# Attention on one core: a rounded one-pass product for the row maxima, exact scores by keys, and the maxima brought in by small transfers

## The chip, the cores and the metric

The kernel runs on one core of a Trainium2 chip. A core has TensorE (PE, the matrix engine, with its weight loads PEld), VectorE (DVE), ScalarE (ACT), GpSimd (POOL) and SyncE (SP, which here only issues transfers), and 16 DMA engines. The metric is device time in microseconds of one execution, the median of several runs. The profiles are one execution each.

## The reference, cut to what matters

Two layers of a streaming encoder over 512 tokens of width 1024. Each layer is a half-weighted SwiGLU block, a mixing stage, a second SwiGLU block and a norm. The change is in the mixing stage, in the attention:

```
q = rms_norm(c_q) @ w_uq            # 8 heads of 64 + 32 (rotary)
kv = rms_norm(c_kv) @ w_ukv         # 8 heads of 64 (keys) + 64 (values)
q, k = rope(rms_norm(q)), rope(rms_norm(concat(k_nope, k_pe)))
for i in range(4):                  # blocks of 128 queries, keys up to the block's end
    scores = (q_i @ k.T) * 96 ** -0.5
    scores = where(chunk(key) <= chunk(query), scores, -1e30)   # chunks of 64 tokens
    out_i = softmax(scores) @ v
x = x + concat(attention, conv) @ w_out
```

Beside the attention runs a conv module: a gated product of 512 channels, a causal depthwise convolution of 31 taps, a layer norm over the channels and a swish. Its output is the other half of the input of `w_out`.

## The kernel before

Activations lie features by tokens: 128 partitions of features, 512 tokens along the free dimension. Most products are split: each float32 operand is cast to a rounded form (`FR`, the "hi") and the rest (the "lo"), and `mm3` (lines 151 to 154) sums hi x hi, hi x lo and lo x hi in PSUM. The mixing stage (`mix_body`, from line 609) works in this order in the code: two conv input groups, latents of queries and keys, `queries` and `keys` (which leave q and kn as tokens x heads x 100 numbers, 96 features and 4 marks for the mask), then the attention, then the conv taps, the layer norm and the output projection.

Attention goes head by head through five stages with a lag each, from `ORDER = "t0s1p3v4o5"` (lines 58 and 874): in step n come `turn(n)`, `scores(n-1)`, `turn_p(n-3)`, `values(n-4)` and `turn_out(n-5)`.

- `turn` transposes q and kn of a head on PE (lines 804, 809), and ScalarE and VectorE scale them out of PSUM as plain float32 (lines 806, 811).
- `scores` multiplies them in float32 with queries as rows: four blocks of 128 queries by 128, 256, 384 and 512 keys (line 824). VectorE takes each row's negated maximum (line 825), ScalarE the exponential with that maximum as bias (line 829). The marks add -1e30 where a query may not see a key.
- `turn_p` transposes the ten 128x128 blocks of the probabilities on PE (line 843); VectorE copies two of the three results out, ScalarE one (line 846, `EVP = "DAD"`).
- `values` multiplies by the values and a column of ones in float32 (line 854), VectorE divides (lines 860, 861).
- `turn_out` turns two heads at a time back and splits them into hi and lo (lines 871, 872, 158, 159).

The convolution has four channel groups (`CONV = "DAAD"`): two are 30 multiply-adds each on VectorE (line 894), two are 30 products on ScalarE (line 898) that POOL adds (line 902). Most of POOL's adds are queued behind the last step of `keys`. POOL then sums the four groups (lines 916 to 918); a product with `onesm` on PE (line 920) gives the mean, and the layer norm follows (lines 924 to 939: VectorE subtracts and adds squares, PE sums at line 190, POOL takes a power at line 170, PE spreads the result at line 208, VectorE and ScalarE finish, and the result is split). The output projection takes eight output groups; the attention half of the first three (`WOG`) is done in `early_groups` (lines 908 to 912), with weights of the first four loaded ahead (`WOP`).

The code fixes what is computed on which engine. The order in which each engine meets its instructions is made by the tile framework's scheduler: it takes ready instructions by their place in the code, with its own estimate of times and with the buffers that are free (seven PSUM banks, 40 slots of the ring that holds q, k and probabilities). `tc.issue_after(ins)` holds instructions of a block behind `ins` where both are on the same engine; `early_groups` is held behind `heads[H - 1]["s"]`, the last score matmul.

Of the kernel before, what the change touches and what calls it, by code (L numbers as in the profile page):

```python
# [7 lines left out]
FP = mybir.dt.float32  # L8
FR = mybir.dt.float32r
BF = mybir.dt.bfloat16  # L10
I32 = mybir.dt.int32
AF = mybir.ActivationFunctionType
ALU = mybir.AluOpType
AX = mybir.AxisListType

P = 128
D = 1024
S = 512
L = 2
KD = D // P  # L20
NT = S // P
H = 8
DN = 64
DR = 32
DQ = DN + DR
DM = DQ + 4
DV = 64
QL = 384
KVL = 256
# [14 lines left out]
LATE = ((), (), (), (0, 1, 2, 3), (4, 5, 6, 7))  # L44
SEQ = "q0 R c1 q1 q2 qo k kt tt uq uk c2"
POOLW = "wo"
QFOLD = 0
EARLY = "s"
PRELOAD = 1
WARM = 8  # L50
# [3 lines left out]
E3 = 3  # L54
WOG = 3
WOP = 4
EVP = "DAD"
ORDER = "t0s1p3v4o5"

VECS = [("g1", 8), ("gm", 8), ("g2", 8), ("gp", 8), ("gql", 3), ("gkl", 2),  # L60
        ("cw", 4 * CK), ("cb", 4), ("lg", 4), ("lb", 4), ("gq", 1), ("gk", 1)]
# [11 lines left out]
def encoder_kernel(ctx: ExitStack, tc: tile.TileContext, xT, consts, vecs, rgain, wgu1, wd1,  # L73
                   wcv, wql, wkl, wuq, wkv, wout, wgu2, wd2, wend, gend, out):
    nc = tc.nc
    PSUM = bass.MemoryType.PSUM
    cpool = ctx.enter_context(tc.tile_pool(name="const", bufs=1))
# [4 lines left out]
    small = ctx.enter_context(tc.tile_pool(name="small", bufs=2))  # L82
# [4 lines left out]
    def nm(s):  # L87
        uid[0] += 1
        return f"{s}{uid[0]}"

    def slot(dt=FP, w=S):
        return ring.tile([P, w], dt, tag="r", name=nm("r"))

    def tmp(w=S, dt=FP):
        return tmps.tile([P, w], dt, tag="t", name=nm("t"))

    def bank():
        return psum.tile([P, S], FP, tag="ps", name=nm("ps"))

    def tiny(tag, w, dt=FP):  # L100
        return small.tile([P, w], dt, tag=tag, name=nm(tag))

    V, A, G, T = nc.vector, nc.scalar, nc.gpsimd, nc.tensor
# [7 lines left out]
    ident = cst[:, CID:CID + P]  # L111
# [11 lines left out]
    V.memset(minus_half, -0.5)  # L123
    onesm = cpool.tile([P, P], FP, name="onesm")
    V.memset(onesm, 1.0 / CW)
    marks = cpool.tile([P, 2, NT, NT], FP, name="marks")
    G.memset(marks, 0.0)
    for t in range(NT):
        G.memset(marks[0:64, 0, t, t:t + 1], 1.0)
        G.memset(marks[64:P, 1, t, t:t + 1], -1e30)  # L130

    def vv(l, name):
        o, w = VOFF[name]
        return vec[:, l, o:o + w]
# [16 lines left out]
    def mm3(o, lh, ll, rh, rl, first, last, free=False):  # L151
        T.matmul(o, lh, rh, start=first, stop=False, skip_group_check=free)  # L152
        T.matmul(o, lh, rl, start=False, stop=False, skip_group_check=free)  # L153
        T.matmul(o, ll, rh, start=False, stop=last, skip_group_check=free)  # L154
# [7 lines left out]
    def split_scaled(src, scale, w=S, p=P):  # L162
        hi, lo = slot(FR, w), slot(FR, w)
        A.activation(hi[:p], src, AF.Copy, scale=scale)
        V.scalar_tensor_tensor(lo[:p], src, scale, hi[:p].bitcast(FP), ALU.mult, ALU.subtract)
        return hi, lo

    def rsqrt(y, ve):

        return G.tensor_tensor(y, ve, minus_half[:, 0:y.shape[1]], ALU.pow).ins  # L170
# [434 lines left out]
    def mix(l, gx, norm, done):  # L605
        with tc.tile_pool(name="k", bufs=4) as kpool:
            mix_body(kpool, l, gx, norm, done)

    def mix_body(kpool, l, gx, norm, done):
# [24 lines left out]
        cqT, ckT, pq, scqs = [], [], [], []  # L634
# [4 lines left out]
        ck = kpool.tile([P, NT, KW], FP, tag="ck", name=nm("ck"), bufs=1)  # L639
        q = kpool.tile([P, NT, H, DM], FP, tag="q", name=nm("q"), bufs=1)  # L640
        kn = kpool.tile([P, NT, H, DM], FP, tag="kn", name=nm("kn"), bufs=1)
        for side, v in enumerate((q, kn)):
            G.tensor_copy(v[:, :, :, DQ:DM], marks[:, side, :, None, :].to_broadcast([P, NT, H, NT]))
        cq, wkl_, sk, ckc, ratio = (tiny(n, NT) for n in ("cq", "wkl", "sk", "ckc", "ratio"))
        ssh = small.tile([P, NT, H], FP, tag="ssh", name=nm("ssh"))
        ssk = small.tile([P, NT, H], FP, tag="ssk", name=nm("ssk"))
# [78 lines left out]
        def queries():  # L725
            wq = [load_w(wuq[l, :, k * 768:(k + 1) * 768], 768, "uq") for k in range(3)]
            for t in range(NT):
                for hf in range(2):
                    hs = slice(hf * 4, hf * 4 + 4)
                    ps = bank()  # L730
                    for k in range(3):
                        ts_ = slice(t * P, (t + 1) * P)
                        cs = slice(hf * 384, (hf + 1) * 384)
                        mm3(ps[:, :384], cqT[k][0][:, ts_], cqT[k][1][:, ts_],
                            wq[k][0][:, cs], wq[k][1][:, cs], k == 0, k == 2)
                    A.copy(q[:, t, hs, 0:DQ], ps[:, :384].rearrange("p (h d) -> p h d", h=4))
                    j = tmp()
                    A.activation(j[:, :384], ps[:, :384], AF.Square)
                    V.tensor_reduce(ssh[:, t, hs], j[:, :384].rearrange("p (h d) -> p h d", h=4),
                                    axis=AX.X, op=ALU.add)  # L740
                V.tensor_scalar(ssh[:, t], ssh[:, t], cq[:, t:t + 1], None, ALU.add)
                scq = small.tile([P, H], FP, tag="scq", name=nm("scq"), bufs=5)
                rsqrt(scq, ssh[:, t])
                scqs.append(scq)
                if t % 2:
                    rope(q[:, t - 1:t + 1, :, DN:DQ], tabs[0][:, :, t - 1:t + 1], H)
                    if not QFOLD:
                        for i in (t - 1, t):
                            V.tensor_tensor(q[:, i, :, 0:DQ], q[:, i, :, 0:DQ], scqs[i][:, :, None].to_broadcast([P, H, DQ]),
                                            ALU.mult)  # L750

        def keys():
            wk = [load_w(wkv[l, :, k * WC:(k + 1) * WC], WC, "uk") for k in range(2)]
# [41 lines left out]
        at = []  # L795
        gq, gk = vv(l, "gq")[0:DM], vv(l, "gk")[0:DM]
        gqs = tiny("gqs", 1)
        V.tensor_scalar(gqs[0:DM], gq, DQ ** 0.5, None, ALU.mult)
        heads = [{} for _ in range(H)]

        def turn(h):
            ps = bank()
            for t in range(NT):
                T.transpose(ps[0:DM, t * P:(t + 1) * P], q[:, t, h], ident)
            qT = slot()
            A.activation(qT[0:DM], ps[0:DM], AF.Copy, scale=gqs[0:DM])
            ps = bank()
            for t in range(NT):
                T.transpose(ps[0:DM, t * P:(t + 1) * P], kn[:, t, h], ident)
            kT = slot()  # L810
            V.tensor_scalar(kT[0:DM], ps[0:DM], gk, None, ALU.mult)
            heads[h]["qk"] = qT, kT

        def scores(h):
            qT, kT = heads[h]["qk"]
            b01, b2, b3 = bank(), bank(), bank()
            mx = small.tile([P, NT], FP, tag="mx", name=nm("mx"), bufs=3)
            pi = []
            ps = [slot() for _ in range(3)]
            ps = [ps[0][:, 0:128], ps[0][:, 128:384], ps[1][:, 0:384], ps[2]]  # L820
            for i in range(NT):
                n = (i + 1) * P
                o = (b01[:, 0:128], b01[:, 128:384], b2[:, 0:384], b3)[i]
                heads[h]["s"] = T.matmul(o, qT[0:DM, i * P:(i + 1) * P], kT[0:DM, 0:n], start=True, stop=True).ins  # L824
                V.tensor_reduce(mx[:, i:i + 1], o, axis=AX.X, op=ALU.max, negate=True)
                p = ps[i]
                if QFOLD:
                    V.tensor_tensor(mx[:, i:i + 1], mx[:, i:i + 1], scqs[i][:, h:h + 1], ALU.mult)
                A.activation(p, o, AF.Exp, bias=mx[:, i:i + 1], scale=scqs[i][:, h:h + 1] if QFOLD else 1.0)  # L829
                pi.append(p)  # L830
            heads[h]["p"] = pi

        def turn_p(h):

            pi = heads[h]["p"]
            pt = []
            for js, eng in (((0,), EVP[0]), ((1, 3), EVP[1]), ((2,), EVP[2])):
                ps = bank()
                sb = slot()
                o = 0  # L840
                for j in js:
                    for i in range(j, NT):
                        heads[h]["t"] = T.transpose(ps[:, o:o + P], pi[i][:, j * P:(j + 1) * P], ident).ins  # L843
                        o += P
                    pt.append((j, sb[:, o - (NT - j) * P:o]))
                (A.copy if eng == "A" else V.tensor_copy)(sb[:, 0:o], ps[:, 0:o])
            heads[h]["pt"] = [p for _, p in sorted(pt, key=lambda e: e[0])]

        def values(h):

# [13 lines left out]
        def turn_out(h):  # L864
# [6 lines left out]
                T.transpose(ps[:, t * P:(t + 1) * P], o[:, t * P:(t + 1) * P], ident)  # L871
            at.append(split(ps))

        STAGES = [({"t": turn, "s": scores, "p": turn_p, "v": values, "o": turn_out}[c], int(d)) for c, d in zip(ORDER[::2], ORDER[1::2])]
        for step in range(H + 6):
            for stage, lag in STAGES:
                if 0 <= step - lag < H:
# [8 lines left out]
        for c in range(4):  # L886
# [4 lines left out]
            for k in range(CK - 2, -1, -1):  # L891
                s = CK - 1 - k
# [35 lines left out]
        r = st.token(CW)  # L928
# [5 lines left out]
        for c in range(4):  # L934
            z = tmp()
            V.tensor_tensor(z, ys[c], pr, ALU.mult)
            s = tmp()
# [4 lines left out]
        for m0 in range(0, KD, WOG):  # L942
            ms = range(m0, min(m0 + WOG, KD))
            os = [bank() for _ in ms] if m0 else early
# [217 lines left out]
```

## Time and profile before

| | |
|---|---|
| median of 3 runs | 1765.05 us (1764.64 to 1766.71) |
| profiled execution | 1766.88 us, span 1765.1 us |
| TensorE busy | 1745.7 us, 8102 matmuls |
| VectorE busy | 1400.8 us |
| ScalarE busy | 942.5 us |
| GpSimd busy | 271.4 us |
| mean granted TensorE clock | 0.997 |

The span runs from the first to the last instruction on the core; the 1.8 us beside it lie around it. Times in the views are counted from the span's start. The attention of layer 0 lies between about 435 and 503 us, that of layer 1 between about 1309 and 1377. A plain float32 matmul stands in the profile as two instructions, a rounded one as one. [...] A row of the groups gives line, engine, operation, output and inputs, shapes and count, then busy time and mean duration in ns, then the idle time ahead of it and what ended that.

### The profile page before, as it was taken

To read this page: it belongs to the slowest core of one execution; us is meant where nothing else is said; L and a number is where in the kernel's file an instruction comes from. 1 tells how busy PE (TensorE), PEld (TensorE's weight loads), DVE (VectorE), ACT (ScalarE), POOL (GpSimd) and SP (SyncE) were. 2 spreads that over 40 slices of the span, in tenths; PEclk is the share of its full clock that TensorE was granted. 3 is DMA by queue.
4 is the path that set the end of the run, shared out by engine and by line. 5 is a ranking of instruction groups with operands and counts; after the bars stand their busy time and mean duration, and the time that the engine had idled before them with its cause. 6 is when DMAs were issued, how large, how long until landed. Compare 5 with 4: busy or idle time off the path is not lost.

```text
span 1765.1 us, 22117 instructions
## 1 busy us (share of the span) xinstructions
PE 1745.7 (99%) x8102; PEld 1448.1 (82%) x8102; DVE 1400.8 (79%) x2033; ACT 942.5 (53%) x1420; POOL 271.4 (15%) x234
## 2 busy tenths in 40 slices
PE   9999999999999999999999999999999999999998
PEld 7888888888788888888888888888887888888886
DVE  8967878679869877869799778866889698678884
ACT  7544445457955544445555344444679455344453
POOL 2000000048942000000000000000579400000000
PEclk9999999999999999999999999999999999999999
DMA  9354434424225355352924445343251444544345
GB/s 294 129 179 138 139 119 122 141 76 123 60 108 132 129 158 167 96 167 83 293 89 142 145 132 167 95 144 107 79 137 31 147 106 136 174 143 145 106 134 153
DMA packets 121917, 236.70 MB, mean 134 GB/s; under 512 B 10705, under 2 KB 58321, under 8 KB 121809
## 3 DMA queue, kind: packets, MB, share of 16 engines
q1 hardware_dynamic: 117488, 222.08, 39.3%
q0 software_dynamic: 3456, 12.58, 3.9%
q8 instruction: 63, 1.03, 0.2%
q10 hardware_dynamic: 864, 0.64, 0.1%
q14 instruction: 46, 0.37, 0.1%
HBM read 207.99 MB, written 25.17 MB: 132 GB/s over the span
## 4 chain that ended last, share of the span: by engine, by line
PE 83%; DMA 6%; DVE 4%; ACT 2%; POOL 2%; issue 2%; SPq 1%; POOLq 0%; ACTq 0%; DVEq 0%
PE ps L154 26%; PE ps L152 26%; PE ps L153 26%; PE ps L854 2%; DMA fr<-in_wgu 2%; POOL y L902 1%; DVE wl L239 1%; DMA raw<-in_wgu 1%; PE ps L824 1%; DMA d<-e 1%; DMA r<-d 1%; PE ps L843 1%; ACT pr L898 1%; DVE fr L336 0%; ACT r L829 0%
## 5 line engine op out<-in xcount | busy, mean ns | idle before, releaser
L153 PE MATMUL ps<-wl,r 128*128 128x512 f32 (+2 forms) x1434 | 548.5, 384 | 1.4 <-DVE wl L239 1.4
L154 PE MATMUL ps<-wh,r 128*128 128x512 f32 (+2 forms) x1434 | 545.6, 384 | 0.2 <-DVE r L265 0.2
L152 PE MATMUL ps<-wh,r 128*128 128x512 f32 (+2 forms) x1434 | 530.2, 385 | 2.2 <-ACT wh L237 1.7
L237 ACT CAST wh<-fr 128x1024 fp32r<-128x1024 f32 x255 | 267.1, 1049 | 237.6 <-PE ps L153 108.6
L154 PE MATMUL ps<-r,wl 128*128 128x512 f32 x944 | 366.3, 390 | 0.7 <-POOL wl L147 0.5
L153 PE MATMUL ps<-r,wh 128*128 128x512 f32 x944 | 366.2, 390 | 0.0
L152 PE MATMUL ps<-r,wh 128*128 128x512 f32 x944 | 362.4, 393 | 1.1 <-ACT r L394 0.3
L239 DVE TENSOR_TENSOR wl<-fr,wh 128x1024 fp32r<-128x1024 f32 x255 | 310.1, 1219 | 52.0 <-ACT wh L237 51.0
L152 PEld LDWEIGHTS ps<-wh,r 128*128 128x128 f32 x1434 | 270.1, 189 | 55.2 <-ACT wh L237 2.6
L153 PEld LDWEIGHTS ps<-wl,r 128*128 128x128 f32 x1434 | 269.9, 188 | 53.9 <-DVE wl L239 1.9
L154 PEld LDWEIGHTS ps<-wh,r 128*128 128x128 f32 x1434 | 269.8, 188 | 52.4 <-DVE r L265 0.6
L141 ACT CAST wh<-raw 128x1024 fp32r<-128x1024 f32 (+2 forms) x142 | 139.7, 989 | 216.4 <-PE ps L153 96.5
L152 PEld LDWEIGHTS ps<-r,wh 128*128 128x128 f32 x944 | 177.1, 188 | 41.2 <-ACT r L394 1.7
L154 PEld LDWEIGHTS ps<-r,wl 128*128 128x128 f32 x944 | 177.2, 188 | 38.9 <-POOL wl L147 1.3
L153 PEld LDWEIGHTS ps<-r,wh 128*128 128x128 f32 x944 | 177.3, 188 | 38.4 <-issue 1.4
L147 DVE TENSOR_TENSOR wl<-raw,wh 128x1024 fp32r<-128x1024 f32 (+3 forms) x126 | 145.9, 1159 | 76.4 <-ACT wh L141 75.6
L902 POOL TENSOR_TENSOR y<-y,pr 128x511 f32<-128x511 f32 (+14 forms) x120 | 158.4, 1320 | 51.1 <-ACT pr L898 43.6
L336 DVE TENSOR_TENSOR fr<-fr,fr 128x1024 f32<-128x1024 f32 x112 | 136.6, 1220 | 12.6 <-DMA fr<-in_wgu 12.6
L484 DVE TENSOR_TENSOR x<-ps,x 128x512 f32<-128x512 f32 x120 | 81.5, 686 | 54.4 <-PE ps L154 54.1
L366 ACT ACTIVATE e<-e,rtok 128x256 f32<-128x256 f32 x120 | 59.9, 507 | 79.1 <-DVE e L357 78.4
L898 ACT ACTIVATE pr<-r,vec 128x511 f32<-128x511 f32 (+14 forms) x120 | 85.0, 734 | 13.7 <-POOL y L902 13.7
L395 DVE TENSOR_TENSOR r<-r,r 128x512 fp32r<-128x512 f32 x88 | 58.0, 681 | 41.5 <-ACT r L394 41.4
(197 smaller groups left out, 1668.2 us busy)
## 6 DMA issues: line engine op xcount, KB each, us to landing
fr<-in_wgu SPq DMA_DIRECT2D x175, 512.0 KB, 4.2
raw<-in_wd SPq DMA_DIRECT2D x56, 512.0 KB, 4.3
d<-e SPq DMA_DIRECT2D x176, 128.0 KB, 3.1
r<-d SPq DMA_DIRECT2D x88, 256.0 KB, 3.2
raw<-in_wd SPq DMA_DIRECT2D x32, 384.0 KB, 3.9
raw<-in_wcv SPq DMA_DIRECT2D x16, 512.0 KB, 3.3
raw<-in_wout SPq DMA_DIRECT2D x16, 512.0 KB, 4.1
raw<-in_wgu SPq DMA_DIRECT2D x8, 512.0 KB, 8.8
```

Source lines behind the costliest of these rows:

```text
L141: A.copy(hi[:, :w], raw[:, :w])
L147: (G if kind in POOLW.split() else V).tensor_tensor(lo[:, :w], raw[:, :w], hi[:, :w].bitcast(FP), ALU.subtract)
L152: T.matmul(o, lh, rh, start=first, stop=False, skip_group_check=free)
L153: T.matmul(o, lh, rl, start=False, stop=False, skip_group_check=free)
L154: T.matmul(o, ll, rh, start=False, stop=last, skip_group_check=free)
L237: order["cast"] = A.copy(hi[:, :w], src[:, :w]).ins
L239: V.tensor_tensor(lo[:, :w], src[:, :w], hi[:, :w].bitcast(FP), ALU.subtract)
L336: V.tensor_tensor(oh, ah, bh, ALU.add)
L366: A.activation(out[j][:, :h], src[j][:, :h], AF.Silu, scale=r)
L484: V.tensor_tensor(xm, pd.rearrange("p (a t j) -> p t a j", a=4, t=NT), xm, ALU.add)
L898: A.activation(pr[:, s:], u[c][:, :S - s], AF.Copy, scale=tap(k))
L902: order["conv"] = G.tensor_tensor(acc[:, s:], acc[:, s:], pr[:, s:], ALU.add).ins
```

## The change

`turn` now splits q and k of a head into hi and lo (four ring slots a head instead of two). A new stage `maxima` multiplies only the hi parts, queries as rows, and VectorE takes the row maxima as before, into a 128x32 tile; a 32x32 VectorE transpose turns this, and four small transfers on SP's queue put the 512 negated maxima as a 101st row into the hi part of the queries, where the keys have a row of ones. `scores` then multiplies keys by queries in three rounded passes, so that the maxima are subtracted in the product and the result has keys as rows: its exponentials, in three ScalarE instructions, are what `values` reads. `turn_p` and its copies are gone. The stages become t0 m1 s2 v3 o4. `heads[h]["s"]` is now the last exponential.

```
-DM = DQ + 4
+DM = DQ + 5
+MAXROW = DM - 1
-EVP = "DAD"
-ORDER = "t0s1p3v4o5"
+ORDER = "t0m1s2v3o4"
...
-    marks = cpool.tile([P, 2, NT, NT], FP, name="marks")
+    marks = cpool.tile([P, 2, NT, DM - DQ], FP, name="marks")
     G.memset(marks, 0.0)
+    G.memset(marks[:, 1, :, NT:NT + 1], 1.0)
+    mx = cpool.tile([P, 32], FR, name="mx")
+    G.memset(mx.bitcast(FP), 0.0)
...
         def turn(h):
-            ps = bank()
-            for t in range(NT):
-                T.transpose(ps[0:DM, t * P:(t + 1) * P], q[:, t, h], ident)
-            qT = slot()
-            A.activation(qT[0:DM], ps[0:DM], AF.Copy, scale=gqs[0:DM])
-            ps = bank()
-            for t in range(NT):
-                T.transpose(ps[0:DM, t * P:(t + 1) * P], kn[:, t, h], ident)
-            kT = slot()
-            V.tensor_scalar(kT[0:DM], ps[0:DM], gk, None, ALU.mult)
-            heads[h]["qk"] = qT, kT
+            qk = []
+            for v, g in ((q, gqs[0:DM]), (kn, gk)):
+                ps = bank()
+                for t in range(NT):
+                    T.transpose(ps[0:DM, t * P:(t + 1) * P], v[:, t, h], ident)
+                qk.append(split_scaled(ps[0:DM], g, p=DM))
+            heads[h]["qk"] = qk
+
+        def maxima(h):
+
+            (qh, _), (kh, _) = heads[h]["qk"]
+            b01, b2, b3 = bank(), bank(), bank()
+            for i, o in enumerate((b01[:, 0:128], b01[:, 128:384], b2[:, 0:384], b3)):
+                T.matmul(o, qh[0:DM, i * P:(i + 1) * P], kh[0:DM, 0:(i + 1) * P], start=True, stop=True)
+                V.tensor_reduce(mx[:, i:i + 1], o, axis=AX.X, op=ALU.max, negate=True)
+            mt = small.tile([P, 32], FP, tag="mt", name=nm("mt"))
+            V.transpose(mt, mx.bitcast(FP))
+            row = qh.bitcast(FP)[MAXROW:DM].rearrange("o (t g r) -> o t g r", t=NT, g=4)
+            for g in range(4):
+                nc.sync.dma_start(out=row[:, :, g], in_=mt[g * 32:g * 32 + NT])
 
         def scores(h):
-            qT, kT = heads[h]["qk"]
...
-                heads[h]["s"] = T.matmul(o, qT[0:DM, i * P:(i + 1) * P], kT[0:DM, 0:n], start=True, stop=True).ins
-                V.tensor_reduce(mx[:, i:i + 1], o, axis=AX.X, op=ALU.max, negate=True)
...
-                A.activation(p, o, AF.Exp, bias=mx[:, i:i + 1], scale=scqs[i][:, h:h + 1] if QFOLD else 1.0)
...
-        def turn_p(h):
...
+            (qh, ql), (kh, kl) = heads[h]["qk"]
+            b0, b13, b2 = bank(), bank(), bank()
+            os = (b0, b13[:, 0:384], b2[:, 0:256], b13[:, 384:512])
+            for j in (0, 1, 3, 2):
+                c = slice(j * P, (j + 1) * P)
+                mm3(os[j], kh[0:DM, c], kl[0:DM, c], qh[0:DM, j * P:S], ql[0:DM, j * P:S], True, True)
+            p0, p13, p2 = slot(), slot(), slot()
+            for p, o in ((p0, b0), (p13, b13), (p2[:, 0:256], b2[:, 0:256])):
+                heads[h]["s"] = A.activation(p, o, AF.Exp).ins
+            heads[h]["pt"] = [p0, p13[:, 0:384], p2[:, 0:256], p13[:, 384:512]]
```

A switch that was off (`QFOLD`) is removed from the code with it.

More of the change, by code (lines that the diff above doesn't have):

```diff
@@ L46 @@
 POOLW = "wo"
-QFOLD = 0
 EARLY = "s"
@@ L642, in mix_body @@
         for side, v in enumerate((q, kn)):
-            G.tensor_copy(v[:, :, :, DQ:DM], marks[:, side, :, None, :].to_broadcast([P, NT, H, NT]))
+            G.tensor_copy(v[:, :, :, DQ:DM], marks[:, side, :, None, :].to_broadcast([P, NT, H, DM - DQ]))
         cq, wkl_, sk, ckc, ratio = (tiny(n, NT) for n in ("cq", "wkl", "sk", "ckc", "ratio"))
@@ L746, in queries @@
                     rope(q[:, t - 1:t + 1, :, DN:DQ], tabs[0][:, :, t - 1:t + 1], H)
[L747 to L750, printed above, removed]
+                    for i in (t - 1, t):
+                        V.tensor_tensor(q[:, i, :, 0:DQ], q[:, i, :, 0:DQ], scqs[i][:, :, None].to_broadcast([P, H, DQ]),
+                                        ALU.mult)
         def keys():
@@ L814, in scores @@
-        def scores(h):
-            qT, kT = heads[h]["qk"]
[L816 to L828, printed above, removed]
-                A.activation(p, o, AF.Exp, bias=mx[:, i:i + 1], scale=scqs[i][:, h:h + 1] if QFOLD else 1.0)
-                pi.append(p)
-            heads[h]["p"] = pi
@@ L833, in turn_p @@
-        def turn_p(h):
[L835 to L847, printed above, removed]
+            qk = []
@@ L872, in turn_out @@
             at.append(split(ps))
-        STAGES = [({"t": turn, "s": scores, "p": turn_p, "v": values, "o": turn_out}[c], int(d)) for c, d in zip(ORDER[::2], ORDER[1::2])]
+        STAGES = [({"t": turn, "m": maxima, "s": scores, "v": values, "o": turn_out}[c], int(d)) for c, d in zip(ORDER[::2], ORDER[1::2])]
         for step in range(H + 6):
```

## The prediction

> **What bounds the kernel now.** I read the page first, for the engine that is never free.
>
> ```profile
> span 1765.1 us, 22117 instructions
> ...
> PE 1745.7 (99%) x8102; PEld 1448.1 (82%) x8102; DVE 1400.8 (79%) x2033; ACT 942.5 (53%) x1420; POOL 271.4 (15%) x234
> ```
>
> TensorE is busy for all but some 19 us of the span, so work taken from it looks like time. But POOL's 15% is an average: the change touches only the attention stage, and there the view of busy time by stretches reads otherwise. Three stretches of layer 0 (start of the score products, body, attention's end to the first products of the conv rows), then the body in layer 1; the columns are the stretch, its length, and busy time of PE, PEld, DVE, ACT and POOL.
>
> ```profile
> 448.40:463.00 14.60, 12.83 (x65) 8.38 (x64) 13.23 (x26) 14.60 (x27) 12.61 (x11) 1.00 0.54 110
> 463.00:502.50 39.50, 38.67 (x302) 34.84 (x300) 38.14 (x81) 32.95 (x63) 37.03 (x31) 1.00 0.01 1
> 502.50:517.10 14.60, 14.44 (x64) 10.97 (x64) 8.32 (x14) 6.41 (x11) 1.54 (x2) 1.00 0.01 1
> 1333.00:1376.00 43.00, 42.16 (x317) 36.98 (x318) 41.67 (x88) 36.43 (x69) 40.39 (x33) 1.00 0.00 1
> ```
>
> In the body PE, DVE and POOL are all busy for 94 to 98% of it, in both layers. So I asked each when it gets through. POOL's order of time (start, length, line, count):
>
> ```profile
> 464.90 34.19 POOL L902 TENSOR_TENSOR y<-y,pr 128x507 f32<-128x507 f32 x26 [0.28 <-ACT pr L898]
> ...
> 501.74 1.26 POOL L918 TENSOR_TENSOR t<-t,r 128x512 f32<-128x512 f32 x1
> ```
>
> The 26 conv adds follow each other at 34.19/26 = 1.315 us, and the last addition of the channel sum ends at 501.74 + 1.26 = 503.00. TensorE's and VectorE's ends:
>
> ```profile
> 502.50 0.63 PE L871 MATMUL ps<-cst,t 128*128 128x128 f32 x4 [0.83 <-DVE t L861]
> 503.06 1.13 PE L920 MATMUL ps<-t,onesm 128*128 128x512 f32 x2
> ```
> ```profile
> 499.29 0.72 DVE L894 SCALAR_TENSOR_TENSOR cv<-r,vec,cv 128x482 f32<-128x482 f32 x1
> ```
>
> Attention's last transposes end at 503.1, where line 920 takes up the channel sum 0.06 us after POOL has it; VectorE's last tap ends at 500.0. The layer norm behind line 920 then takes until
>
> ```profile
> 517.11 1.20 PE L152 MATMUL ps<-r,wh 128*128 128x512 f32 x4 [0.17 <-ACT r L158]
> ```
>
> and PE fills 14.44 of those 14.60 us, mostly with output-projection products of the attention rows: four weights are loaded ahead (WOP), each with 4 blocks of 3 products, 48 in all. So two chains reach 517.1 together: PE's queue, and POOL's conv sum followed by the norm. A cut in PE alone moves only the first.
>
> **TensorE's part.** The chain of waits in order of time gives one head's old work:
>
> ```profile
> 468.01 1.73 PE ps L824 x6
> 469.74 1.09 PE ps L843 x10
> ...
> 473.01 0.49 PE ps L824 x2
> ```
>
> Scores 1.73 + 0.49 and ten transposes 1.09: 3.31 us a head. In their place come one pass of rounded products (maxima) and three (scores), each over 128 + 256 + 384 + 512 columns. Rounded products of 384 and 512 columns stand in the queries and keys:
>
> ```profile
> 413.66 0.33 PE L154 MATMUL ps<-wh,r 128*128 128x384 f32 x1
> 413.83 0.39 PE L152 MATMUL ps<-wh,r 128*128 128x512 f32 x1
> 414.06 0.40 PE L153 MATMUL ps<-wl,r 128*128 128x512 f32 x1
> ```
>
> Start to start that is 0.17 and 0.23. 256 and 128 columns aren't in the trace: at the least half and a third of those (0.115, 0.057), at the most 0.17 each. I take 0.12 and 0.11, the latter as a 128-column transpose above. One pass is 0.63, four 2.52 (2.29 to 2.96); a head saves 0.79 (0.35 to 1.02), eight heads 6.3 us, two layers 12.6. This is what the change would be worth if PE decided. It doesn't.
>
> **VectorE's and ScalarE's part.** From the body's groups and from the lines' own durations (minimum, median, maximum in ns):
>
> ```profile
> L825 DVE TENSOR_REDUCE mx<-ps 128x1 f32<-128x384 f32 (+3 forms) x19 | 9.0, 498 | 0.1
> L846 DVE COPY r<-ps 128x512 f32<-128x512 f32 (+1 forms) x14 | 7.2, 554 | 0.0
> ```
> ```profile
> L811 DVE TENSOR_SCALAR r<-ps,vec x16: 740/743/751, 440.0 to 1355.7; 100x512 f32<-100x512 f32 x16
> ```
> ```profile
> L165 DVE SCALAR_TENSOR_TENSOR r<-ps,vec,r x10: 734/740/750, 379.7 to 1285.4; 128x512 fp32r<-128x512 f32 x10
> ```
> ```profile
> L530 DVE STREAM_TRANSPOSE fr<-x x32: 270/281/291, 1716.9 to 1722.9; 128x128 f32<-128x128 f32 x32
> ```
> ```profile
> L164 ACT ACTIVATE r<-ps,vec x10: 672/678/862, 376.9 to 1283.7; 128x512 fp32r<-128x512 f32 x10
> ```
> ```profile
> L846 ACT COPY r<-ps 128x512 f32<-128x512 f32 x7 | 4.3, 614 | 0.7 <-PE ps L843 0.7
> ```
>
> VectorE loses line 811 (0.74) and two copies (2 x 0.554), gains two lower halves (2 x 0.74) and a 128x32 transpose (under 0.28): 1.85 against at most 1.76, so its end stays near 500. The four reductions remain. ScalarE loses a copy (0.61), gains the keys' upper half (0.68); the exponentials cover the same 1280 columns in three instructions instead of four. Both come out even, nearly 3 us ahead of POOL on VectorE's side.
>
> **POOL's part, which sets the end.** No conv add is removed. What can move it is its feed:
>
> ```profile
> POOL y L902 <- ACT pr L898: 2.3, 5, 0.9
> ```
>
> Between 434 and 504 it waits 2.3 us in five waits for ScalarE's taps, the last of them the 0.28 in POOL's first row above. Exponentials stood ahead of those taps; now they come later, since they wait for a row of maxima. At best the 2.3 vanish. Against that, the upper halves of two heads' keys (2 x 0.68 = 1.4) now stand ahead of the taps there. Between -2.3 and +1.4 I take the middle, -0.5.
>
> **The norm.** Two of its PE steps queue behind at-row products today:
>
> ```profile
> 506.77 2.28 DVE L185 TENSOR_TENSOR acc<-acc,t 128x512 f32<-128x512 f32 x3
> ```
> ```profile
> 509.51 0.95 PE L190 MATMUL ps<-ones,acc 128*128 128x1 f32 x8
> ```
> ```profile
> 511.81 0.69 DVE L204 TENSOR_TENSOR t<-cst,rtok 128x512 f32<-128x512 f32 x1 [1.15 <-POOL rtok L170]
> ```
> ```profile
> 513.19 1.02 PE L208 MATMUL ps<-t,ones 128*128 128x512 f32 x2
> ```
>
> Their inputs are there at 509.05 and 512.50: 0.46 + 0.69 = 1.15 us of queueing. With PE ahead of its work it can go; between 0 and 1.15 I take 0.7.
>
> **The row of maxima.** Four transfers a head wait on SP for the transpose. Behind them on SP stands nothing that is due:
>
> ```profile
> 422.05 29.24 SPq L139 DMA_DIRECT2D raw<-in_wout  x7
> 516.22 4.25 SPq L326 DMA_DIRECT2D fr<-in_wgu  x9
> ```
>
> SP is empty from 451.3 to 516.2, and DMA's share in the body is 0.01. That costs nothing unless attention runs past 516. No 2 KB transfer is in the trace; the nearest on this queue is the turned activations' (issue times in ns, then landing):
>
> ```profile
> L382 SPq DMA_DIRECT2D d<-e x176: 302/452/1698, 39.5 to 1720.3; - x176
> ```
> ```profile
> DMA to landing us min/median/max: 2.0/3.1/6.0
> ```
>
> From the reductions to the row: 4 x 0.498 + a transpose of up to 0.28 + four issues + a landing: 5.3 (4 x 0.30, 2.0, 0.1) to 7.2 us (4 x 0.45, 3.1). Waiting for it are PE's score products, then the exponentials on ScalarE with conv taps queued behind them. The row is small, so I lean to the short end. [...]
>
> The change has a side effect. The early output-projection groups are queued behind heads[7]["s"], but only instructions on that instruction's own engine are held. It was a matmul and becomes an exponential on ScalarE, so these matmuls are held no more: they can fill PE's gaps as soon as rows are there, and may sit on three of the seven PSUM banks while attention still runs. That costs nothing if they run late, and lengthens a head's step if not (second rival).
>
> **Sum.** Per layer -0.5 - 0.7 = -1.2 us, and PE's 6.3 turns into waiting. Two layers: -2.4. The profiled execution took 1766.88, which gives 1764.5; it lies 1.83 above the median of the runs, so against 1765.05 I forecast **1762.7 us**.
>
> **Rivals.**
> [...]
>
> [...]
>
> [...]
>
> *Slower: late rows.* Scores follow maxima by one stage. If a step can't be shorter than the row's chain, 7.2 us and some 0.2 for the first product, eight steps take 59.2 from 448.4: attention ends at 507.6 instead of 503.1, with line 920 queued behind it. That is +4.5 a layer, 1774. It decides above (503.1 - 448.4)/8 = 6.8 us a step; held banks push the same way. Against it: the short end, 5.3.
>
> *All slack comes back.* POOL's 2.3 and the norm's 1.15 both go: 3.45 a layer, 1758.2. More than that POOL's adds don't allow.
>
> *It doesn't do what it says*: were the products of under 512 columns dearer than my bounds, PE would save less, but PE isn't what the sum rests on.
>
> **How the numbers follow.** About 0.2% (3.5 us) is what a measurement of this kernel can tell from no change. Forecast 0.45 (a third of it beyond -3.5), clock 0.22 (0.13 of it slower, 0.09 within), late rows 0.18, all slack 0.15. Faster 0.15 + 0.15 = 0.30, within 0.30 + 0.09 = 0.39, slower 0.13 + 0.18 = 0.31. The range reaches from the third rival, 1758, to the second, 1774; left out are worse delays and a broken estimate of POOL's feed.
>
> **What would show it.** Right: line 902's 26 adds still at 1.3 us, line 918 ending between 500.5 and 504 in layer 0, PE's busy time some 12 us lower, and a new wait of PE for line 158 ahead of the conv rows of 4 us or more in both layers. [...] Late rows: long waits of PE's score products for transfers, and line 918 done before attention's last transposes. Wrong: POOL's last add before 496, or a kernel faster by 7 us and more; then POOL wasn't the floor.

## The result and the profile after

The median went from 1765.47 us to 1794.12 us, ratio 1.0166 (95% interval 1.0136 to 1.0196): slower by 28.7 us, where 1762.7 had been forecast and the range had ended at 1774. The profiled execution took 1794.61 us. Among the experiments, one execution of e17_before_cut took twice its usual time and was the profiled one; no row of it is used.

The top of the page after:

```profile
span 1792.8 us, 22217 instructions
...
PE 1750.2 (98%) x8070; PEld 1461.2 (81%) x8070; DVE 1401.7 (78%) x2033; ACT 940.4 (52%) x1404; POOL 271.2 (15%) x236
```

TensorE has less work and is busy 4.5 us longer than before: part of it must run slower. The ends that the prediction used, in TensorE's order of time:

```profile
516.30 0.63 PE L858 MATMUL ps<-cst,t 128*128 128x128 f32 x4 [0.82 <-DVE t L848]
516.76 1.02 PE L907 MATMUL ps<-t,onesm 128*128 128x512 f32 x2
...
530.66 1.19 PE L154 MATMUL ps<-r,wh 128*128 128x512 f32 x4
```

The channel sum (line 920 before, 907 now) starts at 516.76 instead of 503.06, the conv rows at 530.66 instead of 517.11. From the one to the other it takes 13.90 us, before 14.05: the norm is as it was. All of the 13.55 us is in the attention, and layer 1 has 14.8 us more of the same kind. The stretch of layer 0's attention, before and after, in the columns that the prediction explained:

```profile
448.37:503.06 54.69, 52.10 (x370) 43.63 (x368) 51.37 (x106) 47.58 (x89) 50.17 (x41) 1.00 0.15 30
```
```profile
447.07:516.76 69.69, 55.60 (x353) 50.64 (x352) 50.32 (x104) 47.07 (x82) 51.16 (x42) 0.85 0.13 29
```

TensorE's idle time is 69.69 - 55.60 = 14.09 us against 2.59 (11.5 more), and its busy time 3.5 us more, at a mean granted clock of 0.85. What it waits for, over both layers:

```profile
PE ps L154 <- DMA r<-mt: 20.5, 8, 6.9
PE ps L816 <- DVE mx L817: 5.2, 8, 1.0
```

The first line is new: score products waiting for the row of maxima, 20.5 us in eight waits. Cut at the borders that the clock record itself has (every 3.41 us), the start of the attention reads:

```profile
448.87:452.29 3.42, 1.65 (x5) 0.68 (x4) 3.33 (x8) 3.42 (x6) 3.26 (x4) 1.00 0.92 196
452.29:455.70 3.41, 0.00 (x0) 0.00 (x0) 3.38 (x8) 2.77 (x5) 3.25 (x4) 0.50 0.95 201
455.70:459.11 3.41, 1.24 (x3) 1.08 (x4) 3.27 (x5) 0.90 (x2) 3.41 (x4) 0.50 0.26 50
459.11:462.53 3.42, 3.42 (x15) 3.32 (x15) 1.02 (x2) 2.68 (x5) 2.37 (x3) 0.50 0.00 0
...
469.35:472.77 3.42, 1.05 (x4) 0.79 (x5) 3.42 (x8) 2.10 (x4) 3.18 (x4) 1.00 0.01 1
472.77:476.18 3.41, 3.41 (x17) 3.31 (x15) 3.11 (x6) 2.53 (x5) 3.10 (x3) 0.50 0.02 5
476.18:479.59 3.41, 3.41 (x17) 3.41 (x17) 0.00 (x0) 0.84 (x2) 2.47 (x2) 0.50 0.00 0
479.59:483.01 3.42, 3.42 (x14) 3.13 (x14) 2.53 (x6) 2.46 (x4) 1.07 (x1) 0.50 0.00 0
```

A stretch in which TensorE was busy for 1.65 or 1.05 of 3.41 us is followed by a spell of 10.24 us (three stretches) at half clock, twice in this layer. In the two it does 0 + 1.24 + 3.42 and 10.24 = 14.90 us of busy time at 0.50, where 512-column products start 0.43 us apart (458.44, 458.86, 459.29) against 0.23 at full clock (463.42, 463.65, 463.88). An estimate from these two: 14.90 x (1 - 0.23/0.43), some 7 us lost. So the attention's +15.0 us is about 11.5 (idle) + 7 (half clock) - 3.5 (work saved). The two waits that begin it:

```profile
457.87 0.77 PE L154 MATMUL ps<-r,r 101*128 101x512 f32 x1 [6.09 <-DMA r<-mt]
472.10 0.47 PE L154 MATMUL ps<-r,r 101*128 101x512 f32 x1 [2.03 <-DMA r<-mt]
```

Behind the second lies this chain: VectorE's rows, then SyncE's issues (duration in ns, least, median and most, of the 32 in this layer) and the last two of this head's four.

```profile
464.02 0.74 DVE L817 TENSOR_REDUCE mx<-ps 128x1 fp32r<-128x128 f32 x2
464.68 0.74 DVE L881 SCALAR_TENSOR_TENSOR cv<-r,vec,cv 128x503 f32<-128x503 f32 x1
465.33 0.68 DVE L817 TENSOR_REDUCE mx<-ps 128x1 fp32r<-128x512 f32 x1
...
467.23 0.42 DVE L817 TENSOR_REDUCE mx<-ps 128x1 fp32r<-128x256 f32 x1
...
468.21 0.20 DVE L819 STREAM_TRANSPOSE mt<-mx 128x32 f32<-128x32 f32 x1
```
```profile
L822 SPq DMA_DIRECT2D r<-mt x32: 572/573/753, 451.1 to 506.8; - x32
```
```profile
469.79 1.19 SPq L822 DMA_DIRECT2D r<-mt  x2
```

The reductions of one head are spread from 464.02 to the transpose at 468.21, 4.2 us for 2 us of work, since conv taps (line 881) and splits stand between them on VectorE; then four issues of mostly 0.573 us, done at 469.79 + 1.19 = 470.98; the product starts 1.1 us later. From first reduction to first product 472.10 - 464.02 = 8.1 us. The first head's chain is longer still: in the same orders of time its reductions start at 448.47 and its product at 457.87, 9.4 us, with DMA's share at 0.92 and 0.95 in the first two stretches above. This wait and its counterpart in layer 1 (6.88 us) are 13.0 of the 20.5 us.

POOL and ScalarE are pulled along: the exponentials wait for the late scores, the taps behind them come late, and POOL starves.

```profile
481.94 2.58 POOL L889 TENSOR_TENSOR y<-y,pr 128x496 f32<-128x496 f32 x2 [2.83 <-ACT pr L885]
...
505.66 1.27 POOL L905 TENSOR_TENSOR t<-t,r 128x512 f32<-128x512 f32 x1
```

Its channel sum ends at 506.93 instead of 503.00, but that is 9.8 us ahead of attention's end: POOL no longer decides.

### The profile page after: what moved, and what is told of

The parts are those of the page before. It is cut to its first block, busy times and chain, and to the rows that moved or that the text cites. A ratio compares the mean times of both kernels' runs of the same rounds, so it can differ in the third digit from the quotient of the medians.

```text
span 1792.8 us, 22217 instructions
## 1 busy us (share of the span) xinstructions
PE 1750.2 (98%) x8070; PEld 1461.2 (81%) x8070; DVE 1401.7 (78%) x2033; ACT 940.4 (52%) x1404; POOL 271.2 (15%) x236
## 4 chain that ended last, share of the span: by engine, by line
PE 82%; DVE 5%; DMA 3%; ACT 3%; POOL 2%; issue 2%; SPq 1%; POOLq 0%; ACTq 0%; DVEq 0%
PE ps L154 27%; PE ps L156 26%; PE ps L155 26%; PE ps L841 2%; POOL y L889 1%; DMA fr<-in_wgu 1%; DMA r<-mt 1%; ACT pr L885 1%; DVE wl L241 1%; SPq L822 1%; DMA raw<-in_wd 1%; ACT r L166 0%; DVE wl L149 0%; DVE fr L338 0%; PE ps L192 0%
## 5 line engine op out<-in xcount | busy, mean ns | idle before, releaser
L889 POOL TENSOR_TENSOR y<-y,pr 128x509 f32<-128x509 f32 (+15 forms) x120 | 158.1, 1320 | 59.1 <-ACT pr L885 52.8
L881 DVE SCALAR_TENSOR_TENSOR cv<-r,vec,cv 128x511 f32<-128x511 f32 (+14 forms) x120 | 88.0, 733 | 3.6 <-ACT cv L877 1.7
```

The costliest lines, as they stand in the source:

```text
L881: V.scalar_tensor_tensor(acc[:, s:], u[c][:, :S - s], tap(k), acc[:, s:], ALU.mult, ALU.add)
L889: order["conv"] = G.tensor_tensor(acc[:, s:], acc[:, s:], pr[:, s:], ALU.add).ins
```

## The experiments

Theory: the rows of maxima come late, TensorE stands still for them (20.5 us in eight waits), and the clock falls to 0.50 behind waits such as those that left 1.65 and 1.05 us busy of 3.42; without both, POOL's sum holds the time where it was. Rivals: the new products cost more than counted; the waits matter and the clock doesn't; the rows' landing time is all, or none, of it. The ratio is that to the kernel before in the same set of runs.

### Without rows

**e1_no_rows** leaves the four transfers out; the maxima are computed, not subtracted.

```diff
-            for g in range(4):
-                nc.sync.dma_start(out=row[:, :, g], in_=mt[g * 32:g * 32 + NT])
...
+                heads[h]["s"] = A.activation(p, o, AF.Exp, scale=1e-3).ins
```

> Leaves out the four transfers a head (the maxima are computed but not subtracted, and the exponentials are scaled by 0.001 to stay finite); all else is the changed kernel. Theory 'late rows' (what was lost comes from score products that wait for the row, and from the clock that falls meanwhile): 1758 to 1766 us, granted clock back to 0.997, PE's last attention transposes before 503 in layer 0 and POOL's last sum near 503, so that POOL's floor is what is left. Rival 'dearer work' (the three passes and the upper and lower halves cost PE or the others more than what they replace): stays above 1780 us with the clock at 0.99 or better. Rival 'PE is the bound after all': 1750 to 1755 us, since PE's saving of 5 to 6 us a layer then comes through.

1771.96 us, ratio 1.0034 (1.0023 to 1.0045). 22 of the 28 us are gone with the rows, so the products aren't what is slow. What is left stands at attention's end:

```profile
500.30 1.26 POOL L902 TENSOR_TENSOR t<-t,y 128x512 f32<-128x512 f32 x1
501.64 1.26 POOL L903 TENSOR_TENSOR t<-t,r 128x512 f32<-128x512 f32 x1
```
```profile
499.05 0.63 PE L856 MATMUL ps<-cst,t 128*128 128x128 f32 x4 [2.17 <-DVE t L846]
502.96 2.07 PE L905 MATMUL ps<-t,onesm 128*128 128x512 f32 x2 [3.28 <-POOL t L903]
```
```profile
497.53:500.95 3.42, 0.63 (x4) 0.42 (x4) 1.99 (x5) 1.80 (x3) 3.26 (x4) 1.00 0.00 0
500.95:504.36 3.41, 1.40 (x3) 0.84 (x3) 0.07 (x1) 0.85 (x2) 1.87 (x2) 0.50 0.00 0
```

Attention is over at 499.7 and TensorE waits 3.28 us for POOL, whose sum ends at 502.90 (before 503.00): the predicted floor. The waits leave 0.63 us busy of 3.42, and the granted clock is 0.50 from 500.95 until 507.8, in layer 1 for 10.24 us.

**e7_nr_fill**: the same with idle products (a constant tile multiplied with itself) in those two waits.

```diff
+                with tc.issue_after(order["v"]):
+                    idle(9)
...
+                with tc.issue_after(order["to"]):
+                    idle(13)
```

> As e1_no_rows (row transfers left out, maxima not subtracted, exponentials scaled by 0.001), with 9 idle products put behind the last head's value products and 13 behind the last transposes, so that TensorE runs while it waits for POOL's channel sum; nothing else moves. By the clock (mine): the channel sum comes at the same time (503), but the stretches at half clock at 501 to 508 and 1375 to 1385 vanish, and the time falls from 1772 by 2.4 to 3 us a layer to 1765.5 to 1768. Rival, the wait itself and the products queued behind it are the cost: 1771 to 1774.

1765.82 us, ratio 1.0001 (0.9992 to 1.0011). The sum comes when it came, and the stretch at half clock is gone in both layers:

```profile
497.95:501.36 3.41, 3.41 (x31) 3.22 (x30) 1.55 (x3) 2.37 (x3) 3.25 (x3) 1.00 0.00 0
501.36:504.77 3.41, 2.94 (x16) 2.11 (x15) 0.72 (x2) 0.28 (x2) 1.40 (x2) 1.00 0.00 0
```

Work that computes nothing took 6.1 us off. The clock is shown as a cause, and so is the floor: with neither late rows nor half clock the kernel stands where it stood before.

**e13_nr_gap**: e7 with 4 products instead of 13 in the second place.

> As e7_nr_fill (row transfers left out, maxima not subtracted, exponentials scaled by 0.001, idle products at the end of attention), but with 4 idle products instead of 13 behind the last transposes, so that TensorE has one wait of about 2.6 us for POOL's sum. By busy time in a 3.41 us stretch (mine: under some 2.0 us busy the next stretch is at half clock): whether it falls hangs on how the wait lies in the stretches; if it falls in both layers, 1768 to 1771, if in one, 1766.5 to 1769. [...]

1768.01 us, ratio 1.0011 (1.0002 to 1.0020), executions from 1764.2 to 1770.6. One wait of 2.45 us is left in each layer, and in the profiled execution the stretch behind it is at 0.50 in layer 0 and at 1.00 in layer 1:

```profile
497.85:501.26 3.41, 1.11 (x3) 0.63 (x4) 0.30 (x1) 1.08 (x2) 2.17 (x2) 1.00 0.00 0
501.26:504.67 3.41, 3.41 (x10) 2.62 (x9) 3.25 (x6) 2.43 (x4) 0.00 (x0) 0.50 0.00 0
...
1371.66:1375.07 3.41, 1.56 (x5) 0.99 (x6) 0.39 (x1) 0.63 (x2) 1.72 (x2) 1.00 0.00 0
1375.07:1378.48 3.41, 3.41 (x17) 2.79 (x16) 3.31 (x6) 2.43 (x4) 0.00 (x0) 1.00 0.00 0
```

So one wait of 2.45 us in one piece was followed by half clock and the other wasn't. What the half clock cost isn't shown here, since the profiled execution is the fastest of the ten. Nor does the busy time left in the stretch decide alone: 1.56 us kept the full clock here, 1.65 lost it in the kernel after (448.87).

**e8_nr_early**: e1 with `E1 = 1`, one early output group ahead of the channel-sum product.

> As e1_no_rows, with the first of the three early output groups ahead of the channel-sum product on TensorE instead of behind it (12 products of 0.23 us, 2.8 us in each layer). If what the kernel without row waits loses is the in-order wait for POOL and the clock that falls in it (mine): the 3.3 us wait is filled, the time falls by 5 to 10 us from 1772 to 1762 to 1767. Rival, after the channel sum the norm's chain decides, so moved products only make a hole later: 1770 to 1774.

1772.28 us, ratio 1.0035 (1.0024 to 1.0047): no gain, as the rival has it. The group's first products run at half clock (0.50 from 500.46 to 503.87; the 2.2 us wait ahead of them stays), the sum's product moves from 502.96 to 505.44 behind them, and a new wait of 2.1 us appears ahead of the norm's sums. The hole only moves along TensorE's queue. The time alone wouldn't settle it: the profiled execution, the slowest of six, also has 10.24 us at half clock from 1333.31, at the attention's start in layer 1, which e1 doesn't have.

### With rows, waits moved or filled

**e2_fill**: 26 idle products ahead of the first head's scores, 9 ahead of the third's.

> The changed kernel with idle products put on PE where it waits for the first head's row (26, some 5.7 us) and for the third head's (9, some 2 us), so that PE is busy but nothing it computes is used. Theory 'the clock' (half rate over some 20 us a layer is the larger part of the loss): clock near 0.997 and 1778 to 1783 us, that is 11 to 16 us better than the changed kernel. Rival 'the waits' (PE waits the same time, the low clock mostly covers time in which it would wait anyway): clock near 0.997 but 1788 to 1795 us.

1795.13 us, ratio 1.0159 (1.0083 to 1.0235). Only two executions, 1800.65 (profiled) and 1789.62. Waits for rows fall from 20.5 to 7.5 us and the first spells at half clock go, but nothing is won: a stretch with a later wait of 1.36 us and 1.99 us busy is followed by 34 us at 0.50, though TensorE then is busy for 97% of them.

```profile
487.53:490.94 3.41, 1.99 (x10) 1.31 (x9) 3.41 (x9) 2.74 (x6) 3.18 (x4) 1.00 0.00 1
490.94:525.08 34.14, 33.04 (x135) 30.70 (x134) 11.23 (x25) 10.86 (x20) 9.52 (x8) 0.50 0.00 1
```

**e4_conv_late**: the last conv input group (`conv_in(3)`) behind the first maxima instead of the second turn.

> The changed kernel with the fourth conv input group moved in the code from behind the second head's turn to behind the first head's maxima, so that the first row travels while PE has 11 us of other work. Theory 'late rows': the wait of about 6 us for the first row is gone and with it the first low clock; 1775 to 1783 us, with the later waits of 1 to 2 us a head left. Rival 'transfers queue behind weights' (the first row is late because of weight loads in flight): the first row still lands 6 us after its issue, but PE does not wait for it; same time by this run, told apart by the landing. Rival 'dearer work': 1788 us or more.

1831.58 us, ratio 1.0365 (1.0314 to 1.0416): a miss. That group's products had covered ScalarE's and VectorE's split of the first head; without it TensorE stood still for a whole stretch (438.74 to 442.15), maxima then waited 11.4 us for splits over both layers, and seven spells at half clock, 119 us in all, followed.

**e5_both**: the same, with scores three steps behind the turn (`ORDER = "t0m1s3v4o5"`).

> The same, and the scores one stage later (t0 m1 s3 v4 o5), so that each row has two steps. Theory 'late rows': no wait for rows, clock 0.997, 1758 to 1767 us, at POOL's floor or a little above. Rival 'steps are set by something else' (VectorE's queue, PSUM banks, the ring): waits move from rows to VectorE's reductions and the time stays above 1775 us.

1782.81 us, ratio 1.0089 (1.0060 to 1.0118). No wait for a row is left; the 15.7 us that maxima wait for splits, and four spells at half clock, are the price of the moved group.

**e3_lag3**: `ORDER = "t0m1s3v4o5"` alone.

> Only the stages change: score products three steps behind the transposes instead of two, so each row of maxima has one more step to land. Late rows (mine): TensorE's waits for rows after the first head fall from 14 us in both layers to under 2 us, the score products stop giving stretches at half clock from the second head on, and what is left is the first row, then the floor of POOL's adds with TensorE's wait for the channel sum: 1771 to 1782. Rival, it is the work itself (three rounded products of 101 rows and the exponentials by keys are too slow, whatever waits): a stage more changes nothing or costs a step of 6 us a layer, 1790 to 1806.

1768.97 us, ratio 1.0026 (1.0016 to 1.0036), lower than I had expected. One more step for the row takes 25 of the 28.7 us off with every product and transfer in place. Left is mainly the start, with one spell at half clock in each layer (10.24 and 6.83 us):

```profile
453.99 0.79 PE L816 MATMUL ps<-r,r 101*128 101x128 f32 x3 [2.10 <-ACT r L166]
457.45 0.77 PE L154 MATMUL ps<-r,r 101*128 101x512 f32 x1 [2.67 <-DMA r<-mt]
```

**e6_late_wo**: the output projection's 512 KB weight loads held on SyncE behind the second head's row.

```diff
-        with tc.issue_after(order["keys"]):
+        with tc.issue_after(order["keys"]), tc.issue_after(heads[1]["row"]):
```

> The loads of the first output-projection weights are held on SyncE behind the row transfers of the second head (index 1). If the first row lands late because its transfers queue with those 512 KB loads (mine): the first head's wait for its row falls from 6.1 us to under 3 us in layer 0 and likewise in layer 1, one of the two 10.24 us stretches at half clock goes, and the time falls by 6 to 12 us to 1782 to 1788. Rival, the landing time of the small transfers is their own: the wait stays at 5 us or more and the time at 1790 to 1798, or rises if the weights come late.

1813.73 us, ratio 1.0294 (1.0249 to 1.0339). The mechanism shows and the time is worse:

```profile
453.57 0.77 PE L154 MATMUL ps<-r,r 101*128 101x512 f32 x1 [2.43 <-DMA r<-mt]
...
476.62 0.76 PE L154 MATMUL ps<-r,r 101*128 101x512 f32 x1 [10.33 <-DMA r<-mt]
```

Without loads beside it the first row's wait falls from 6.09 to 2.43 us (in layer 1 from 6.88 to 2.41). From the row's first issue to the product 6.78 us become 3.80 (449.77 to 453.57), in layer 1 7.57 become 3.59: 3.0 and 4.0 us were the loads'. The loads, put off, then hit later rows: 10.33 us, with DMA's share at 0.88 to 1.09 from 463.50 to 480.56.

### The full kernel, repaired

**e10_lag3_fill**: e3 with 9 idle products ahead of the third head's maxima, 11 ahead of the first scores, and e7's 9 and 13 at the end.

> The whole computation: score products three steps behind the transposes (as e3_lag3), with idle products where TensorE waits: 9 ahead of the third head's maxima, 11 ahead of the first score products, 9 behind the last value products, 13 behind the last transposes. If late rows and the clock are all that the change loses (mine): no stretch at half clock in the attention of either layer, the channel sum of POOL decides again at about 503, and the time is that of before, 1764 to 1767. Rival, the row transfers cost more than waits (exponentials that come late starve POOL of its taps): POOL's sum ends at 505 or later and the time stays at 1768.5 or more.

1771.25 us, ratio 1.0038 (1.0024 to 1.0052): a miss, by my own idle products. No stretch of the attention is at half clock, but the products run on after POOL's sum, ready at 500.36 + 1.26 = 501.62:

```profile
502.41 0.60 PE L871 MATMUL ps<-cst,t 128*128 128x128 f32 x4
502.85 3.07 PE L122 MATMUL ps<-ones 128*128 128x128 f32 x26
505.75 1.02 PE L923 MATMUL ps<-t,onesm 128*128 128x512 f32 x2
```

**e14_lag3_start** keeps only those at the start.

> The whole computation: score products three steps behind, idle products only at the start of attention (9 ahead of the third head's maxima, 11 ahead of the first score products), none at its end. If the idle products at the end were all that e10_lag3_fill lost (mine): attention ends at about 501.5 instead of 502.9, the channel sum follows at once, the conv rows start some 4 us earlier in each layer, and the time falls to 1762 to 1766, if no stretch at half clock comes back at the end. Rival, it isn't those: 1768.5 to 1772.

1764.79 us against 1766.31, ratio 0.9990 (0.9980 to 0.9999), within what 0.2% lets one tell from no change. Transposes and sum now meet:

```profile
500.52 0.63 PE L866 MATMUL ps<-cst,t 128*128 128x128 f32 x4 [0.82 <-DVE t L856]
501.33 1.95 PE L915 MATMUL ps<-t,onesm 128*128 128x512 f32 x2 [0.18 <-POOL t L913]
```
```profile
498.08:501.50 3.42, 2.41 (x20) 2.07 (x20) 1.30 (x3) 0.86 (x3) 3.04 (x3) 1.00 0.00 0
501.50:504.91 3.41, 3.41 (x7) 2.00 (x8) 2.28 (x4) 2.63 (x5) 0.00 (x0) 0.50 0.00 0
```

One stretch at half clock is left in layer 0 behind these two waits, none in layer 1. With the rows in time and the first waits filled the time is that of before, so late rows, with the clock that they cost, are the loss of the kernel with real rows; the products are not.

**e15_lag3_start_dve**: e14 with POOL's last channel addition on VectorE (`YP = 0`).

> As e14_lag3_start, with the last of POOL's three additions of the channel sum on VectorE (0.68 us there, 1.27 us on POOL). If POOL's sum still ends the stage: 0.5 us a layer less, 1 us in all. If TensorE's last transposes end it: no difference of more than 0.5 us.

1764.64 us, ratio 1.0002 (0.9985 to 1.0018): no difference from before or from e14; eight of ten executions lie at 1762.9 to 1766.0, two at 1774.1 with a lower mean clock (0.994 and 0.993 against 0.997 to 0.999).

**e18_best**: e15 with 5 idle products behind the last value products.

> The whole computation: score products three steps behind, idle products where TensorE waits (9 ahead of the third head's maxima, 11 ahead of the first score products, 5 behind the last value products), POOL's last channel-sum addition on VectorE. If executions over 1765 of e15_lag3_start_dve had a stretch at half clock after the 0.8 us wait at attention's end (mine): they go, and the median is 1762 to 1764.5, below both kernels. Rival, the spread has another cause: median 1764.5 to 1766, with executions over 1770 still there.

1764.89 us, ratio 0.9993 (0.9984 to 1.0002). The median stays, above the 1762 to 1764.5 that I had expected. No execution of eleven is over 1770, where two of ten were in e15; so few don't show that the half clock was their cause. The five products mostly take the place of a wait: from the end of the last value product to the transposes it is 1.01 us (501.30 to 502.31), where it was 0.82 in e15 (499.28 to 500.10). No version with the whole computation beats the kernel before by more than 0.2%.

### Is the saving there when POOL is early?

**e11_pesum** and **e12_before_pesum** replace POOL's three channel additions by four products in one PSUM bank, in e10 (2 idle products left at its very end) and in the kernel before.

```diff
-        T.matmul(pm, onesm, ysum, start=True, stop=True)
+        for c in range(4):
+            T.matmul(pm, onesm, ys[c], start=c == 0, stop=c == 3)
```

> As e10_lag3_fill, but POOL's three additions of the channel sum (3 x 1.27 us a layer) are gone: TensorE sums the four channel groups in one PSUM bank, with four plain products of 0.9 us instead of one; of the last idle products 2 are left. If POOL was the floor that hid TensorE's saving (mine): the mean is there at about 501 to 502 instead of 503.9, and the time falls below before, to 1758 to 1763. Rival, the norm or TensorE itself decides by then: 1764 to 1768.

> The kernel before with the same channel sum on TensorE instead of POOL, nothing else. If TensorE and POOL reach the end of attention together there (mine): POOL's relief can't be used, TensorE has three more products of 0.9 us a layer, and the time rises by 1 to 5 us to 1766.5 to 1770.5. Rival, POOL alone decided: the time falls by 2 to 5 us to 1760.5 to 1763.5.

1780.00 us, ratio 1.0084 (1.0069 to 1.0099), and 1778.08 us, ratio 1.0073 (1.0058 to 1.0088): both misses. All four products were put behind attention's last transposes (in the second kernel from 504.40 to 507.4), and the end of the chain grew instead of shrinking. In the second kernel the conv rows start at 522.17 instead of 517.11, 5.1 us later, and in layer 1 at 1401.21 instead of 1390.55, 10.7 later, about what the profiled execution lost. Of the 5.1 us, 3.7 lie between the sum's first product and the conv rows: three more products, 2.6 us, and a wait of 1.45 us for ScalarE at the end instead of 0.17. They say nothing of the floor.

**e16_nr_cut** and **e17_before_cut** leave out eight of POOL's 60 conv additions in each layer, in e1 and in the kernel before.

```diff
+                if kind == "A" and k < 4:
+                    continue
```

> As e1_no_rows (row transfers left out, maxima not subtracted, exponentials scaled by 0.001), and of POOL's conv additions the last four taps of two channel groups are left out (8 x 1.3 us a layer; ScalarE still makes the products), so that POOL is done 10 us earlier. If POOL was the floor that hid TensorE's saving (mine): the channel sum starts when attention's last transposes end, at 499.7 instead of 503.0, no stretch at half clock follows, and the time falls to 1757 to 1762, 3 us a layer or more under the kernel before with the same cut. Rival, the saving isn't there: within 2 us of that kernel.

> The kernel before with the same eight POOL additions left out in each layer, nothing else. If TensorE reaches the end of attention together with POOL there (mine): POOL's relief is worth next to nothing, 1763 to 1766. Rival, POOL alone decided: attention's end has 4 us of queueing in it and the time falls by 5 us or more, below 1760.5.

1769.31 us, ratio 1.0022 (1.0013 to 1.0031), and 1768.34 us, ratio 1.0014 (1.0004 to 1.0023). Both rose above what I expected. The scheduler had reordered the engines: in e16 more conv taps stand ahead of the splits on ScalarE, TensorE waited 1.2 and 1.0 us for splits at the start and ran 13.7 us at half clock there. The kernel before gets nothing from an early POOL; what makes it 2 us slower is open.

**e19_nr_cut_fill**: e16 with idle products in its waits, 9 at the start and 5 behind the last value products.

> As e16_nr_cut (row transfers, the subtraction of the maxima and eight of POOL's additions a layer left out, exponentials scaled by 0.001), with idle products in TensorE's waits: 9 ahead of the third head's maxima, 5 behind the last value products. If TensorE's saving is real and POOL hid it (mine): no stretch at half clock, attention ends at 500 with POOL done at 498, and the time falls to 1757.5 to 1761.5. Rival, the saving isn't there even with the clock held: 1764 or more.

1758.24 us (all runs within 0.2), ratio 0.9959 (0.9946 to 0.9972): 8.4 us faster, as the theory had it. By this POOL's additions held the time, once rows and clock didn't.

```profile
447.00:498.40 51.40, 50.58 (x380) 46.88 (x378) 48.92 (x104) 44.27 (x80) 41.54 (x34) 1.00 0.17 39
```
```profile
498.40 1.12 PE L915 MATMUL ps<-t,onesm 128*128 128x512 f32 x2 [0.27 <-POOL t L913]
```

Full clock throughout, and the channel sum at 498.40 instead of 503.06, 4.66 us earlier. TensorE's saving comes out when rows, clock and POOL are all out of the way (the rows and eight additions are missing from its work).

## Why the prediction was wrong

- **The failed step: the row's chain, priced at 5.3 to 7.2 us and taken at "the short end", so that the sum has no term for late rows.** The chain took 8.1 us for the third head and 9.4 for the first. The rival's own point, 6.8 us a step, was passed, and both its signs came: score products waiting 20.5 us for transfers, and POOL done 9.8 us ahead of attention. The third head's landing was short: some 1.7 us from the start of the last issue to the product, where the prediction took 2.0 to 3.1. The issues were 4 x 0.573 where I took 0.30 to 0.45 from transfers of another form; and the four reductions, taken back to back at 2 us, took 4.2 us between VectorE's conv taps (read from the rows; no run moves the taps away). The empty SyncE queue was seen rightly, but the 512 KB loads it had issued just before were still moving, which cost the first row 3.0 and 4.0 us more (e6). The prediction's own first row had shown them: DMA's share is 0.54 between 448.40 and 463.00. I read the 0.01 of the body below it.
- **The rivals were kept apart.** Late rows (1774, chance 0.18) and a falling clock (chance 0.22) each had its own world; the one causes the other. With both, 1794; with the rows out, 1772; with the clock held too, 1765.8.
- **The clock's chance, 0.22, had no measured point behind it.** No run shows a length of idleness at which the clock falls: 1.77 us idle, spread over a 3.42 us stretch (448.87), were followed by 0.50, and of two waits of 2.45 us in e13 one was and one wasn't. The four spells of the kernel after lie in the attention, are 6.83 or 10.24 us long and cost by estimate 3 to 4 us each on top of the wait (some 7 us for the two in layer 0; e1 to e7, 6.1 us for two).
- **POOL's floor: right.** Its sum ends at 502.90 (e1) and 502.83 (e7) against 503.00, and e7 stands at the time before. The feed's -0.5 was -0.1 to -0.2.
- **The norm's -0.7: not there.** 14.05 us from channel sum to conv rows before, 13.90 after, 14.05 in e7: the same at-row products stand ahead of the same two steps.
- **TensorE's 0.79 a head: right in full flow, less over a whole layer.** In e7 52.67 us are busy from the first maxima (448.61) to the channel sum (502.89), of which some 5.1 are idle products: 47.6 against 52.10, 4.5 us a layer or 0.57 a head, inside the bounds 0.35 to 1.02; e19's 8.4 us over two layers agree. Where nothing waits, the transposes of q follow each other at 461.48 and 467.12 in e7, 5.64 us a step, and at 466.97 and 473.34 before, 6.37: 0.73 a head. That it doesn't decide was right.
- **VectorE and ScalarE come out even: right** (50.32 and 47.07 us busy against 51.37 and 47.58), but even totals hid how VectorE's order stretches the reductions.
- **Freed early groups: no effect.** The scheduler still put them behind line 907.

## What to carry to other kernels

A new hand-over between engines is priced from first input to first use through every queue that it crosses, with what else stands in them; give it one more pipeline step before judging the products (e3: 25 us). When work leaves TensorE while another engine holds the end, count TensorE's busy time in each stretch of its clock record (3.41 us here): a saving that became waiting turned into a slowdown of 6.1 us in e1 (against e7). A filled wait shows in one run whether the wait or the clock costs, but take the filler out where the wait is not certain (e10).

## What the runs showed of the hardware

In the nineteen traces used, every change of the granted clock lies on a grid of 3.41 us, and where the grid lies against the program differs from trace to trace (the first fall is at 43.97 us in the kernel before and at 42.69 in the kernel after). Counted on that grid, without each kernel's start and tail: of 36 stretches at full clock with TensorE busy for less than 2.0 us, 33 were followed by half clock (not so 1.56 us in e13, 1.94 in e8 and 1.96 in e12); of the thousands above that, four, at 2.13 (e16) to 2.58 (e8). The stretch ahead of half clock was not always idle: 1.76 us of 3.41 were busy in e11 (1331.14), 2.41 in e14 (498.08).

The way back was less regular: from one stretch (e14) to eleven at half clock, up to 37.6 us (e4), with TensorE recorded as busy throughout in most of them; in e2 it was busy for 97% of 34.14 us at 0.50. What decides it stays open.
